# Three small VectorE operations at the end of an attention block moved to GpSimd

## The chip, the cores and the metric

The kernel runs on 1 core of one Trainium2 chip. The metric is device time of one execution in microseconds (us), the median of several executions. Less is better.

## The reference

Two layers of a diffusion backbone run over 2048 latent tokens and 256 context tokens of width 1024. In each layer one input projection is cut into three head groups; two of them are attentions:

- A, windowed attention: 6 query heads in 2 groups of 3, each group with one key and value head. A block of 128 queries sees 3 blocks of latent keys and all 256 context keys, and the softmax has one more term, a learned sink per head.
- C, neighbourhood attention: 6 heads, each query sees a window of 8 rows by 16 columns on a 32 by 64 grid, with a bias, and all context keys. There is no sink.

```python
s_sink = jnp.broadcast_to(sink.reshape(A_KV_HEADS, A_GROUP)[None, None, :, :, None, None], s_win.shape[:-1] + (1,))
p_win, p_ctx, _ = joint_softmax([s_win, s_ctx, s_sink])
o = einsum('bnkgqj,bnjkd->bnqkgd', p_win, vw) + einsum('bnkgqj,bjkd->bnqkgd', p_ctx, v_ctx)
```

Then come an output projection, a LayerNorm and an expert-choice mixture of experts, which the change does not touch.

## The kernel before, in words

Each engine executes its own instructions strictly in the order in which the program was written, and waits on semaphores where it needs another engine's result. `phase_att(l)` (L893) writes the attention of layer l. Its list of blocks is first A: 2 units (key heads) of 16 latent blocks, in the first layer also 2 context blocks each; then C: 6 units (heads) of 4 blocks, in the first layer also one context block each. A block is made of members: 3 heads in A, 4 tiles of queries in C.

The main loop takes one member per turn and writes, with a lag of up to three members between the steps: `qk` (L1040, L1041: scores, TensorE), `soft_max` (L1062: mask or bias added and the minimum taken, VectorE), `soft_exp` (L1070: exponential and its sum `ss`, ScalarE), `trans` and `trans_ctx` (L1087, L1110: transposes, TensorE), copies of the transposes into `ph` (L1199, ScalarE) and their low parts `pl` (L1190, VectorE).

Three turns after a block's last member, the generator `pv` (L1115) begins. It does one piece at each "R" of the orders ORDERA and ORDERC, two per turn: products with the values (L1145), copy to `ot` (L1151), the sink's exponential (L1153 on VectorE: sink minus minimum into `rs`; L1154 on ScalarE), transposes back (L1158), copy to `o` (L1161), the sum `ss` with the sink's term (L1163, VectorE), its reciprocal (L1165, VectorE), the two halves of the product added (L1167, VectorE, reads PSUM), the scaling of `o` (L1170, VectorE), and the store of `o` from SyncE's queue (L1172 for A, L1174 and L1178 for C).

GpSimd has two tasks in attention. For each unit of C it issues 16 small transfers that lay out a table of biases (L960 in `load_unit`), and for three of the four column groups of a unit it makes three tiles of bias from table and mask (L1002 in `bias_part`), after zeroing the two bias buffers once per layer (L990, L994). `load_unit` for the first head of C is written at the fifth block of A's second unit, that for the next head at the second block of the first one.

Of the kernel before, what the change touches and what calls it, by code (L numbers as in the profile page):

```python
# [12 lines left out]
ALU = mybir.AluOpType  # L13
# [211 lines left out]
def build(ctx, tc, t, out):  # L225
    nc = tc.nc
    V, S, P, G, SY = nc.vector, nc.scalar, nc.tensor, nc.gpsimd, nc.sync
# [665 lines left out]
    def phase_att(l):  # L893
# [6 lines left out]
        op = es.enter_context(tc.tile_pool(name="at_o", bufs=6))  # L900
# [12 lines left out]
        sink = sinks[:, l, :]  # L913
# [7 lines left out]
        for b in blist:  # L921
            nm = 3 if b[0] == "A" else (4 if b[2] < 4 else 2)
# [192 lines left out]
        def pv(b, nm):  # L1115

            kind, u, n = b
            rec = st[b]
            ph, pl = rec["ph"], rec["pl"]
            N = 128 * nm  # L1120
            v = units[kind, u]["v"]
            po = pso.tile([128, 512], F32, name="po")
            steps = []
            if kind == "A":
                steps = [(v[:, j, :], slice(9 + 3 * j, 12 + 3 * j), 0, N) for j in range(2)]
                if n >= 2:
                    a0, a1 = max(n - 1, 2), min(n + 1, NT - 1)
                    steps += [(v[:, a0 + j, :], slice(3 * j, 3 * j + 3), 0, N) for j in range(a1 - a0 + 1)]
            else:
                steps = [(v[:, j, :], slice(16 + 4 * j, 16 + 4 * j + nm), 0, N) for j in range(2)]  # L1130
                if n < 4:
                    vw = blks[b]["vw"]
                    for r in range(8):
                        a, z = ((0, 1), (0, 2), (0, 2), (1, 3), (1, 3), (2, 4), (2, 4), (3, 4))[r]
                        s0 = 2 * r + (1 if r == 7 else 0)
                        steps.append((vw[:, r, :], slice(s0, s0 + z - a), 128 * a, 128 * z))
            ns = len(steps)
            work = []
            for x, (w, s, c0, c1) in enumerate(steps):
                work.append((po[:, c0:c1], w, ph[:, s, :], x == 0, False))  # L1140
            for x, (w, s, c0, c1) in enumerate(steps):
                work.append((po[0:64, c0:c1], w[:, 0:64], pl[:, s, :], False, x == ns - 1))
            per = -(-len(work) // PVN[nm])
            for j, (o, w, r, s0, s1) in enumerate(work):
                P.matmul(o, w, r, start=s0, stop=s1, skip_group_check=True)  # L1145
                if j % per == per - 1 and j < len(work) - 1:
                    for _ in range(PVW):
                        yield
            yield
            ot = wp.tile([128, 512], F32, name="ot")  # L1150
            S.copy(ot[:, :N], po[:, :N])  # L1151
            if kind == "A":
                V.tensor_tensor(rec["rs"][:, :nm], sink[:, 3 * u:3 * u + 3], rec["mx"][:, :nm], op=ALU.subtract)  # L1153
                S.activation(rec["rs"][:, :nm], rec["rs"][:, :nm], AF.Exp, scale=-1.0)  # L1154
            yield
            px = pst.tile([128, 4, 128], F32, name="pt")
            for m in range(nm):
                P.transpose(px[:, m, :], ot[:, 128 * m:128 * m + 128], ident)  # L1158
            yield
            o = op.tile([128, 4, 64], F32, name="o")  # L1160
            S.copy(o[:, :nm, :], px[:, :nm, 64:128])  # L1161
            if kind == "A":
                V.tensor_tensor(rec["ss"][:, :nm], rec["ss"][:, :nm], rec["rs"][:, :nm], op=ALU.add)  # L1163
            yield
            V.reciprocal(rec["rs"][:, :nm], rec["ss"][:, :nm])  # L1165
            yield
            V.tensor_tensor(o[:, :nm, :], px[:, :nm, 0:64], o[:, :nm, :], op=ALU.add)  # L1167
            yield
            yield
            V.tensor_tensor(o[:, :nm, :], o[:, :nm, :], rec["rs"][:, :nm, None].to_broadcast([128, nm, 64]), op=ALU.mult)  # L1170
            if kind == "A":
                SY.dma_start(MIXA[l][128 * n:128 * n + 128, 192 * u:192 * u + 192], o[:, 0:3, :].rearrange("p m d -> p (m d)"))  # L1172
            elif n == 4:
                SY.dma_start(MIXC[l][0:256, 64 * u:64 * u + 64].rearrange("(m p) d -> p m d", p=128), o[:, 0:2, :])  # L1174
            else:
                dst = MIXC[l][256:TT, 64 * u:64 * u + 64].rearrange("(m a g b) d -> m g a b d", m=4, a=8, g=4)
                for m in range(4):
                    (G if b == blist[-1] else SY).dma_start(dst[m, n], o[:, m, :])  # L1178
            del st[b], blks[b]
# [3 lines left out]
        for i, (b, m, nm) in enumerate(mem):  # L1183
            kind, u, n = b
# [20 lines left out]
        for i in range(NM + LAG):  # L1205
            b, m, nm = mem[i - LAG]
            win, ctx_ = [], []
            for x in ORDERA if mem[min(i, NM - 1)][0][0] == "A" else ORDERC:
                if x == "R":
                    run()  # L1210
                elif x in "AaDdEe" and i >= LAG:
                    if x == "A":
                        win = trans(i - LAG)
                    elif x == "a":
                        ctx_ = trans_ctx(i - LAG)
                    elif x in "Dd":
                        copies(win if x == "D" else ctx_, b)
                    else:
                        lows(win if x == "E" else ctx_, b)
                elif x == "B" and i < NM:  # L1220
                    qk(i)
                elif x == "C" and 1 <= i <= NM:
                    soft_max(i - 1)
                elif x == "F" and 1 <= i <= NM:
                    soft_exp(i - 1)
            for x in bias_at.get(i, []):
                bias_part(*x)
            if i >= LAG and m == nm - 1:
                gens.append(pv(b, nm))
# [722 lines left out]
```

## Time and profile before

| | |
|---|---|
| runs (us) | 4326.2, 4334.8, 4321.42; median 4326.2 |
| profiled execution | 4323.15 us, span of its trace 4321.4 us |
| TensorE (matmul) busy | 3853.9 us, 89% of the span |
| VectorE busy | 2915.8 us, 67% |
| ScalarE busy | 1999.0 us, 46% |
| GpSimd busy | 783.9 us, 18%, 850 instructions |
| attention, first layer | about 630 to 1073 us from the span's start |
| attention, second layer | about 2788 to 3222 us |

Shares are means over the whole span. A kernel of many stages has a different limit in each, so what counts for a change in attention is read from the two stretches of attention alone. In the rows below PE is TensorE's matmul, PEld its weight load, DVE VectorE, ACT ScalarE, POOL GpSimd, SP SyncE; L-numbers are lines of the kernel before.

### The profile page before, as it was taken

What the parts mean: (1) busy time and instruction counts of PE and PEld (TensorE: products, weight loads), DVE (VectorE), ACT (ScalarE), POOL (GpSimd) and SP (SyncE); (2) the same over time, 40 slices, a digit from 0 to 9 for tenths busy, and PEclk for the clock granted to TensorE, in tenths of its full rate; (3) what the DMA queues carried; (4) which work ended last, traced back from release to release, by engine and by line L of the source; (5) the groups of instructions that cost most, each with busy time, mean ns of one, the idle gap of its engine ahead of it and who ended that gap; (6) DMA issues with size and microseconds to landing.
All of it is one profiled execution on the core that took longest, in us unless ns stands there. A gap on an engine that the chain in (4) does not pass through costs nothing. (4 is left out here: it accounts for less than half of the span.)

```text
span 4321.4 us, 64189 instructions
## 1 busy us (share of the span) xinstructions
PE 3853.9 (89%) x22980; PEld 3285.1 (76%) x22980; DVE 2915.8 (67%) x5836; ACT 1999.0 (46%) x3918; POOL 783.9 (18%) x850
## 2 busy tenths in 40 slices
PE   7999989999998699999978999899989918988893
PEld 5877778888885388888857888788878718888783
DVE  6555549998676366676747665499877756656576
ACT  4344338887332143343425443388763304333344
POOL 0000011052221022222210000111422201111114
PEclk9999989999998899999989999999999959999996
DMA  7666674586644878888857666645865327776796
GB/s 229 172 209 187 198 189 107 118 177 154 235 159 143 189 208 201 204 217 196 223 171 230 192 205 187 171 116 110 169 185 193 131 80 190 195 221 194 217 234 203
DMA packets 897295, 789.94 MB, mean 183 GB/s; under 512 B 125928, under 2 KB 780400, under 8 KB 893136
## 3 DMA queue, kind: packets, MB, share of 16 engines
q1 hardware_dynamic: 855744, 656.83, 56.4%
q0 software_dynamic: 41232, 129.01, 10.6%
q8 instruction: 182, 2.98, 0.3%
q14 instruction: 137, 1.12, 0.1%
HBM read 607.08 MB, written 178.48 MB: 182 GB/s over the span
## 5 line engine op out<-in xcount | busy, mean ns | idle before, releaser
L178 ACT CAST wh<-wraw 128x1024 fp32r<-128x1024 f32 x636 | 655.9, 1048 | 621.9 <-DMA wraw<-in_w_gate 278.2
L186 DVE TENSOR_TENSOR wl<-wraw,wh 128x1024 fp32r<-128x1024 f32 x636 | 754.7, 1217 | 152.2 <-ACT wh L178 152.0
L1190 DVE TENSOR_TENSOR pl<-pt,ph 128x256 fp32r<-128x256 f32 (+2 forms) x792 | 360.2, 495 | 23.0 <-ACT ph L1199 18.4
L1199 ACT CAST ph<-pt 128x256 fp32r<-128x256 f32 (+2 forms) x792 | 308.9, 445 | 99.2 <-PE pt L1087 91.3
L624 PE MATMUL gem<-hh,wh 128*128 128x512 f32 (+1 forms) x960 | 354.5, 369 | 0.0
L625 PE MATMUL gem<-hl,wh 128*128 128x512 f32 (+1 forms) x960 | 352.1, 367 | 0.0
L626 PE MATMUL gem<-hh,wl 128*128 128x512 f32 (+1 forms) x960 | 350.0, 365 | 0.0
L1070 ACT ACTIVATE p<-lg,mx 128x640 f32<-128x640 f32 (+3 forms) x408 | 331.5, 813 | 38.3 <-DVE mx L1062 36.7
L1802 PE MATMUL pa<-xh,wh 128*128 128x288 f32 (+1 forms) x1024 | 317.5, 310 | 0.0
L1804 PE MATMUL pa<-xh,wl 128*128 128x288 f32 (+1 forms) x1024 | 308.3, 301 | 0.8 <-DVE wl L186 0.8
L1803 PE MATMUL pa<-xl,wh 128*128 128x288 f32 (+1 forms) x1024 | 307.3, 300 | 0.0
L1802 PE MATMUL pu<-xh,wh 128*128 128x288 f32 (+1 forms) x1024 | 299.9, 293 | 0.0
L1804 PE MATMUL pu<-xh,wl 128*128 128x288 f32 (+1 forms) x1024 | 294.6, 288 | 0.0
L1803 PE MATMUL pu<-xl,wh 128*128 128x288 f32 (+1 forms) x1024 | 292.6, 286 | 0.0
L1666 POOL DMA_INDIRECT ACC<-y,ix x62 | 150.7, 2430 | 651.7 <-DVE y L1647 334.2
L802 PE MATMUL gem<-wh,hh 128*128 128x512 f32 x544 | 220.7, 406 | 0.6 <-ACT hh L593 0.6
L803 PE MATMUL gem<-wl,hh 128*128 128x512 f32 x544 | 217.6, 400 | 1.4 <-DVE wl L186 1.4
L804 PE MATMUL gem<-wh,hl 128*128 128x512 f32 x544 | 217.0, 399 | 0.0
L1833 PE MATMUL py<-wh,gh 128*128 128x512 f32 x512 | 205.1, 401 | 12.7 <-DVE y L1647 6.1
L1571 PE MATMUL tr<-ident,xe 128*128 128x128 f32 x512 | 89.6, 300 | 139.4 <-DVE xl L1584 91.8
L1802 PEld LDWEIGHTS pa<-xh,wh 128*128 128x128 f32 x1024 | 208.5, 204 | 3.1
L1546 POOL DMA_INDIRECT xe<-H,ix x80 | 98.2, 1228 | 619.9 <-DVE ix L1541 352.9
(352 smaller groups left out, 10103.4 us busy)
## 6 DMA issues: line engine op xcount, KB each, us to landing
wraw<-in_w_in SPq DMA_DIRECT2D x160, 512.0 KB
wraw<-in_w_gate SPq DMA_DIRECT2D x128, 512.0 KB
wraw<-in_w_up SPq DMA_DIRECT2D x128, 512.0 KB
wraw<-in_w_down SPq DMA_DIRECT2D x128, 512.0 KB
wraw<-in_w_mod SPq DMA_DIRECT2D x88, 512.0 KB
k<-KC SPq DMA_DIRECT2D x48, 576.0 KB
vw<-VS SPq DMA_DIRECT2D x192, 128.0 KB
VS<-vs SPq DMA_DIRECT2D x36, 512.0 KB
```

Source lines behind the costliest of these rows:

```text
L178: self.nc.scalar.copy(h, self.raw[i])
L186: self.nc.vector.tensor_tensor(e[1], self.raw[i], e[0].bitcast(F32), op=ALU.subtract)
L624: P.matmul(pg[:, t0:nt], wh[:, cs_], hh[:, k, t0:nt], start=(k == 0), stop=False)
L625: P.matmul(pg[:, t0:nt], wh[:, cs_], hl[:, k, t0:nt], start=False, stop=False)
L626: P.matmul(pg[:, t0:nt], wl[:, cs_], hh[:, k, t0:nt], start=False, stop=(k == KD - 1))
L802: P.matmul(pg, hh[:, k, tk], wh[:, cs_], start=(k == 0), stop=False)
L1070: S.activation(p[:, 0:768 - w0], rec["lg"][:, w0:768], AF.Exp, bias=st[b]["mx"][:, m:m + 1], scale=-1.0, accum_out=st[b]["ss"][:, m:m + 1])
L1190: V.tensor_tensor(view(st[b]["pl"]), src, view(st[b]["ph"].bitcast(F32)), op=ALU.subtract)
L1199: S.copy(view(st[b]["ph"]), src)
L1802: P.matmul(pp, wh[:, cs_], xh[:, k, :], start=(k == 0), stop=False)
L1803: P.matmul(pp, wh[:, cs_], xl[:, k, :], start=False, stop=False)
L1804: P.matmul(pp, wl[:, cs_], xh[:, k, :], start=False, stop=(k == KD - 1))
```

## The change

In `pv` three operations go from VectorE (`V`) to GpSimd (`G`). The first is also written at another place: at the start of `pv` instead of behind the products. All other work is the same.

```diff
             N = 128 * nm
+            if kind == "A":
+                G.tensor_tensor(rec["rs"][:, :nm], sink[:, 3 * u:3 * u + 3], rec["mx"][:, :nm], op=ALU.subtract)
             v = units[kind, u]["v"]
...
             if kind == "A":
-                V.tensor_tensor(rec["rs"][:, :nm], sink[:, 3 * u:3 * u + 3], rec["mx"][:, :nm], op=ALU.subtract)
                 S.activation(rec["rs"][:, :nm], rec["rs"][:, :nm], AF.Exp, scale=-1.0)
...
             if kind == "A":
-                V.tensor_tensor(rec["ss"][:, :nm], rec["ss"][:, :nm], rec["rs"][:, :nm], op=ALU.add)
+                G.tensor_tensor(rec["ss"][:, :nm], rec["ss"][:, :nm], rec["rs"][:, :nm], op=ALU.add)
             yield
             V.reciprocal(rec["rs"][:, :nm], rec["ss"][:, :nm])
...
-            V.tensor_tensor(o[:, :nm, :], o[:, :nm, :], rec["rs"][:, :nm, None].to_broadcast([128, nm, 64]), op=ALU.mult)
+            G.tensor_tensor(o[:, :nm, :], o[:, :nm, :], rec["rs"][:, :nm, None].to_broadcast([128, nm, 64]), op=ALU.mult)
```

In the changed kernel the three stand on L1122, L1164 and L1171; L1163 to L1170 of the kernel before are one line further down. The next pieces show the order in which instructions stand on GpSimd in the first layer. Before, at the start of attention (`toep` is the table of biases, `va` and `bias` the two bias buffers):

```order
L723 DMA OB0_91<-stl_5459 128x257
L960 DMA toep_7362<-in_rpb 8x16x48 x16
L990 MEMSET bias_5510 128x2048
L994 MEMSET va_8579 128x256 x3
L1002 TENSOR_TENSOR va_8579<-maskC_5509,toep_7362 128x384
L1002 TENSOR_TENSOR va_8579<-maskC_5509,toep_7362 128x512
L1002 TENSOR_TENSOR va_8579<-maskC_5509,toep_7362 128x384
L960 DMA toep_8679<-in_rpb 8x16x48 x16
```

Nothing of a block's end stands between these instructions. Now, around the first 16 transfers, in A's second unit (the numbers tell buffers apart: `rs_7059` and `rs_7135` belong to two blocks that follow each other):

```order
L1164 TENSOR_TENSOR ss_7058<-ss_7058,rs_7059 128x3
L1171 TENSOR_TENSOR o_7283<-o_7283,rs_7059 128x192
L960 DMA toep_7362<-in_rpb 8x16x48 x16
L1122 TENSOR_TENSOR rs_7220<-sinks_80,mx_7218 128x3
L1164 TENSOR_TENSOR ss_7134<-ss_7134,rs_7135 128x3
L1171 TENSOR_TENSOR o_7398<-o_7398,rs_7135 128x192
```

The same 16 transfers have moved behind the scaling of one block and ahead of the sum of the next. And now at the end of A in the first layer, where the second 16 transfers stand:

```order
L1164 TENSOR_TENSOR ss_8323<-ss_8323,rs_8324 128x3
L990 MEMSET bias_5510 128x2048
L994 MEMSET va_8580 128x256 x3
L1002 TENSOR_TENSOR va_8580<-maskC_5509,toep_7362 128x384
L1171 TENSOR_TENSOR o_8556<-o_8556,rs_8324 128x192
L1002 TENSOR_TENSOR va_8580<-maskC_5509,toep_7362 128x512
L1122 TENSOR_TENSOR rs_8498<-sinks_80,mx_8496 128x3
L1164 TENSOR_TENSOR ss_8413<-ss_8413,rs_8414 128x3
L1002 TENSOR_TENSOR va_8580<-maskC_5509,toep_7362 128x384
L960 DMA toep_8679<-in_rpb 8x16x48 x16
L1171 TENSOR_TENSOR o_8628<-o_8628,rs_8414 128x192
L1164 TENSOR_TENSOR ss_8497<-ss_8497,rs_8498 128x3
```

Before, the transfers and the bias tiles stood alone on GpSimd. Now they stand between the ends of the blocks; in both layers one group of 16 transfers has sums with the sink (L1164) of A's blocks behind it in A's second unit, and one at the passage from A to C.

## Rows read from the trace of the kernel before

**Rows 1.** Windows: stretch, PE, PEld, DVE, ACT, POOL busy (us), PEclk, DMA share, GB/s

```profile
700.00:750.00 50.00, 49.12 (x343) 43.72 (x342) 49.25 (x163) 45.56 (x142) 7.23 (x12) 1.00 0.24 68
...
3100.00:3150.00 50.00, 45.58 (x324) 41.63 (x323) 42.34 (x98) 38.65 (x96) 24.86 (x32) 0.93 0.81 163
```

**Rows 2.** Timeline of one A block: start us, us, engine, line, operation [idle before <-releaser]

```profile
716.50 0.88 DVE L1062 CUSTOM_DVE_ANT_0 lg<-lg,maskA,sinks 128x640 f32<-128x640 f32 x1
716.66 0.19 PEld L1040 LDWEIGHTS lg<-k,qa 128*128 128x128 f32 x1 [0.16 <-ACT p L1070]
...
716.85 0.23 ACT L1154 ACTIVATE rs<-rs 128x3 f32<-128x3 f32 x1
...
717.30 0.16 DVE L1163 TENSOR_TENSOR ss<-ss,rs 128x3 f32<-128x3 f32 x1
...
718.29 0.17 DVE L1165 RECIPROCAL rs<-ss 128x3 f32<-128x3 f32 x1
...
719.15 0.35 DVE L1167 TENSOR_TENSOR o<-pt,o 128x192 f32<-128x192 f32 x1
...
721.04 0.35 DVE L1170 TENSOR_TENSOR o<-o,rs 128x192 f32<-128x192 f32 x1
...
721.38 0.88 DVE L1190 TENSOR_TENSOR pl<-pt,ph 128x384 fp32r<-128x384 f32 x2
...
722.17 0.89 DVE L1062 CUSTOM_DVE_ANT_0 lg<-lg,maskA,sinks 128x640 f32<-128x640 f32 x1
```

**Rows 3.** Timeline of two C blocks of the second layer, PE and DVE

```profile
3101.83 0.55 PE L1087 MATMUL pt<-ident,p 128*128 128x128 f32 x3
...
3110.14 0.55 PE L1087 MATMUL pt<-ident,p 128*128 128x128 f32 x3
```

```profile
3104.09 1.05 DVE L1170 TENSOR_TENSOR o<-o,rs 128x256 f32<-128x256 f32 x1
...
3112.40 0.42 DVE L1170 TENSOR_TENSOR o<-o,rs 128x256 f32<-128x256 f32 x1
```

**Rows 4.** Timeline: a long L1170 in A, and PE behind it in both layers

```profile
755.30 3.23 DVE L1170 TENSOR_TENSOR o<-o,rs 128x192 f32<-128x192 f32 x1
...
759.92 0.44 PE L1110 MATMUL pt<-ident,p 128*128 128x128 f32 x2 [3.46 <-DVE pl L1190]
...
2902.10 0.44 PE L1110 MATMUL pt<-ident,p 128*128 128x128 f32 x2 [1.75 <-DVE pl L1190]
```

**Rows 5.** Timeline of POOL, first layer of attention

```profile
622.81 4.77 POOL L960 DMA_DIRECT2D toep<-in_rpb  x8
...
636.41 1.82 POOL L990 MEMSET bias<- 128x2048 f32 x1
742.77 0.81 POOL L994 MEMSET va<- 128x256 f32 x3 [104.54 <-PE po L1145]
...
746.72 9.34 POOL L960 DMA_DIRECT2D toep<-in_rpb  x16
```

**Rows 6.** Groups of POOL, by form: count | busy us, mean ns | idle before

```profile
L496 POOL TENSOR_SCALAR m<-m 128x1 f32<-128x1 f32 x68 | 64.3, 946 | 360.8 <-ACT xr L488 360.8
...
L1002 POOL TENSOR_TENSOR va<-maskC,toep 128x384 f32<-128x384 f32 x36 | 36.6, 1016 | 210.9 <-DVE mx L1062 210.9
...
L1002 POOL TENSOR_TENSOR va<-maskC,toep 128x512 f32<-128x512 f32 x18 | 23.1, 1284 | 34.9 <-DVE mx L1062 34.8
```

**Rows 7.** Timeline at the end of A, both layers: ACT and DVE

```profile
834.16 0.21 ACT L1154 ACTIVATE rs<-rs 128x3 f32<-128x3 f32 x1
...
2984.58 0.21 ACT L1154 ACTIVATE rs<-rs 128x3 f32<-128x3 f32 x1
```

```profile
841.44 0.17 DVE L1165 RECIPROCAL rs<-ss 128x3 f32<-128x3 f32 x1
...
2993.10 0.16 DVE L1165 RECIPROCAL rs<-ss 128x3 f32<-128x3 f32 x1
```

## The prediction

> **What bounds the kernel now.** I read the windows of attention first, since the change touches nothing else. In A's stretch VectorE is busy 49.25 of 50 us, TensorE 49.12 and GpSimd 7.23; in C's stretch VectorE has 42.34 and GpSimd 24.86 [rows 1]. So VectorE looks like A's limit and not like C's. A busy TensorE is no proof of a limit, because overlapping matmuls count as busy, so next I read one block in the timeline.
>
> In A, VectorE starts the same member of two blocks at 716.50 and 722.17: a block takes 5.67 us, and between these rows the timeline shows no idle time on VectorE [rows 2]. TensorE's weight loads wait once per block, 0.16 us, for an exponential whose minimum VectorE delivered late [rows 2]. So VectorE is the limit in A, but TensorE follows close behind.
>
> In C, TensorE starts the same transposes at 3101.83 and 3110.14, 8.31 us apart. In the first of these blocks L1170 on VectorE took 1.05 us, in the second 0.42 us [rows 3], and the next block of each kind keeps the same distance. VectorE may lose 0.63 us there without any change of the block's time: in C TensorE is the limit.
>
> GpSimd works ahead. The two groups of 16 transfers in the first layer ran at 622.81 and 746.72 [rows 5], the second nearly 100 us ahead of the first block that needs it. Nothing waited for them.
>
> **What leaves VectorE.** In A each of 68 blocks loses three instructions. By distances of starts, L1170 and L1153 together hold VectorE from 721.04 to 721.38, 0.34 us; L1163 takes 0.16 us by its row [rows 2]. That is 0.50 us per block. This is the upper bound of the gain: 68 x 0.50 = 34 us. The lower bound is TensorE's visible wait, 0.16 us, since without it TensorE is the limit: 60 undisturbed blocks x 0.16 = 10 us. Some short waits of matmuls hide behind weight loads that run ahead, so I take a little above the near end, 0.22 us: **60 x 0.22 = -13.2 us**.
>
> In C 54 blocks lose L1170. Rows 3 show that even its long form costs nothing, so I take **0** there. The bound is the long form's excess of 0.63 us for the 26 L1170 that the timeline shows over 0.5 us in C: -16 us, which rows 3 speak against.
>
> The long form itself is a collision. L1170 reads two tensors in SBUF, and it lasts 3.23 us at 755.30 in place of 0.35 us [rows 4, 2], while GpSimd was making bias tiles. TensorE then waited 3.46 us, and 1.75 us at the like place of the second layer [rows 4]. VectorE's other operations in attention read scores or transposes in PSUM, or one small tensor, so these two waits go: **-5.2 us**.
>
> **What GpSimd gets.** From the tiles of 384 and 512 columns, 1016 and 1284 ns, a column costs 2.1 ns and an instruction 0.21 us at the start [rows 6]. So the scaling costs about 0.61 us for 192 columns and 0.75 us for 256, and each of the two tiny ones 0.22 us; the upper bound for a tiny one is 0.95 us [rows 6]. In an undisturbed block that is 1.05 us of 5.67. Does anyone wait? ScalarE's exponential ends at 717.08, the sum can stand at 717.30, and VectorE asks for it at 718.29 [rows 2]: even at 0.95 us it would be in time. The first operation now stands at the start of `pv` and is early. The scaling can start as soon as L1167 ends, 1.54 us before L1170 started before, so the store is not late. Undisturbed blocks therefore pay **0**.
>
> **What is queued behind the 16 transfers.** This is the wait that the change adds. GpSimd no longer works ahead: each group of 16 transfers now stands behind a block's scaling, and in A the next block's sum stands behind the transfers. VectorE's reciprocal waits for that sum, and minimum and low parts of the following members are queued behind the reciprocal. A group takes 9.34 us, or 13.60 us (622.81 to 636.41) where its transfers must wait for earlier ones to land [rows 5].
>
> Second unit of A, once in each layer, told in times of the block of rows 2: L1167 ends at 719.50, the scaling takes until 720.11, the transfers until 729.45, L1122 and L1164 until 729.89. The reciprocal of the next block is due at 718.29 + 5.67 = 723.96. VectorE stands for 5.9 us, or 10.2 us with the long group. I take 6: **+12 us** for both layers. I stay near the short end though the next head's keys are loaded at the same time, because a wait of TensorE for that load's queue should vanish in the pause.
>
> End of A, first layer: the exponential of one block ends at 834.37 [rows 7]. Behind it GpSimd has L1164 0.22, zeroing 1.82 and 0.81, a tile 1.02, a scaling 0.61, a tile 1.28, L1122 0.22, L1164 0.22, a tile 1.02 (this comes to 841.59), the transfers 9.34, a scaling 0.61 and the L1164 in question 0.22: 851.76. Its reciprocal is due at 841.44 [rows 7]: **+10.3 us**, with the long group 14.6.
>
> End of A, second layer: the exponential ends at 2984.79; L1164 0.22, transfers 9.34, scaling 0.61 and L1164 0.22 make 2995.18, due at 2993.10 [rows 7]: **+2.1 us**, with the long group 6.3.
>
> In C no reciprocal waits for GpSimd, since C has no sink, and the tiles are needed some five members (10 us) after they are written. I take 0, with the last block's scaling of 0.75 in place of 0.36 us in each layer: **+0.8 us**.
>
> **Sum.** -13.2 - 5.2 + 12 + 10.3 + 2.1 + 0.8 = +6.8 us on the profiled execution's 4323.15 us, 4330 us. The median of the runs stands 3.05 us above that execution, so the predicted median is **4333 us**, 0.16% above 4326.2. A measurement of this kernel can tell about 0.3% (13 us) from no change, so the forecast is no measurable change.
>
> A rule of the Trainium skill speaks against the whole idea: GPSIMD Engine Reference, section 4.1 Engine selection, sends elementwise work on tiles to VectorE because GpSimd is about twice as slow with two inputs. Here the 384-column row gives no direct pair, but 1.05 us of GpSimd for 0.50 us of VectorE agrees in size. By that rule alone the change would lose where GpSimd's time is on the path, which is the third rival.
>
> **The rivals.**
> - *VectorE's full share comes out of A* (0.14). If TensorE's waits are all due to VectorE, A's 68 blocks give 34 us in place of 13.2: 4312 us, faster. For it: no idle time of VectorE. Against it: TensorE's 49.12 of 50 us [rows 1].
> - *The transfers take long* (0.22). They are now issued beside the loads of the next head's keys. With 13.6 us each, the four places lose 4.3 us more: +17, 4350 us, slower. It decides from some 11 us per group. For it: the group at 622.81, beside such loads. Against: the one at 746.72.
> - *GpSimd's own slowness is on every block's path* (0.06). If a tiny operation with its two hand-overs takes more than 1.05 us (718.29 less 0.16 less 717.08), VectorE waits in each block; at 1.3 us that is 68 x 0.25 = 17 us: 4350 us, slower.
> - *The change gives A nothing* (0.10), because TensorE is the limit there as in C. Without the 13.2 us it ends at 4346 us, slower.
>
> **How the numbers follow.** The forecast has 0.48; its own spread is 4322 to 4344. The range 4313 to 4351 takes in the full gain of A below and the long transfers above. Faster by over 0.3% (under 4313): 0.14. Slower by over 0.3% (over 4339): the three slower rivals, less what they share with gains elsewhere, 0.34. Within: 0.52.
>
> **What the profile after would show.** In A a block of some 5.45 us; VectorE idle before the minimum or the low parts, TensorE without the 0.16 us wait. No L1170-like operation over 0.5 us on VectorE, no waits of 3.46 and 1.75 us behind it. Four pauses in which VectorE's reciprocal waits for GpSimd's sum, about 6, 10, 6 and 2 us, each behind L960 on GpSimd. C at 8.31 us per block as before. The prediction is wrong if these four pauses are missing, if A's block falls to 5.2 us, or if VectorE waits for GpSimd in every block.

## The result, and the profile after the change

Six runs of the changed kernel gave a median of 4352.8 us (4349.7 to 4355.23), six of the kernel before 4329.82 us: a ratio of 1.0055, interval 1.0041 to 1.0069. The change costs 23 us. The forecast was 4333 us with a range up to 4351. The profiled execution took 4354.22 us, 31.07 us more than the profiled one of before; 8 of these lie in how the two executions stand to their medians. Lines from L1120 on have moved by one or two: L1122 is the subtraction, L1164 the sum, L1166 the reciprocal, L1168 the sum of halves, L1171 the scaling.

First the windows that answer to [rows 1] (stretch, PE, PEld, DVE, ACT, POOL busy, PEclk, DMA share, GB/s):

```profile
700.00:750.00 50.00, 49.37 (x346) 44.25 (x345) 46.73 (x133) 46.09 (x144) 8.12 (x29) 1.00 0.20 60
3100.00:3150.00 50.00, 45.11 (x321) 41.00 (x320) 39.73 (x93) 37.95 (x93) 26.35 (x35) 0.93 0.78 162
```

VectorE is relieved as planned, 46.73 in place of 49.25 us of 50. The timeline of VectorE and of the weight loads shows what an undisturbed block of A makes of it:

```profile
788.68 0.88 DVE L1062 CUSTOM_DVE_ANT_0 lg<-lg,maskA,sinks 128x640 f32<-128x640 f32 x1
...
794.36 0.88 DVE L1062 CUSTOM_DVE_ANT_0 lg<-lg,maskA,sinks 128x640 f32<-128x640 f32 x1
```

```profile
794.63 0.19 PEld L1040 LDWEIGHTS lg<-k,qa 128*128 128x128 f32 x1 [0.17 <-ACT p L1070]
```

The same member comes 5.68 us later, where it was 5.67 us before, and the weight load still waits 0.17 us for an exponential [rows 2]. The freed half microsecond bought nothing. In C the same transposes on TensorE start 8.31 and 8.33 us apart, against 8.31 before [rows 3]:

```profile
3129.28 0.55 PE L1087 MATMUL pt<-ident,p 128*128 128x128 f32 x3
...
3137.59 0.55 PE L1087 MATMUL pt<-ident,p 128*128 128x128 f32 x3
...
3145.92 0.55 PE L1087 MATMUL pt<-ident,p 128*128 128x128 f32 x3
```

The loss is in the reciprocal. The view of line L1166 gives its waits in all, and the timeline of VectorE each of them:

```profile
L1166 DVE RECIPROCAL rs<-ss x122: 155/167/176, 648.7 to 3242.9; 128x3 f32<-128x3 f32 x68, 128x4 f32<-128x4 f32 x48, 128x2 f32<-128x2 f32 x6
its engine sat idle before it (us, times) until:
  POOL ss L1164: 41.8, 5
```

```profile
766.92 0.18 DVE L1166 RECIPROCAL rs<-ss 128x3 f32<-128x3 f32 x1 [12.68 <-POOL ss L1164]
844.74 0.18 DVE L1166 RECIPROCAL rs<-ss 128x3 f32<-128x3 f32 x1 [1.39 <-POOL ss L1164]
859.51 0.18 DVE L1166 RECIPROCAL rs<-ss 128x3 f32<-128x3 f32 x1 [12.56 <-POOL ss L1164]
2933.87 0.17 DVE L1166 RECIPROCAL rs<-ss 128x3 f32<-128x3 f32 x1 [12.23 <-POOL ss L1164]
3017.45 0.18 DVE L1166 RECIPROCAL rs<-ss 128x3 f32<-128x3 f32 x1 [2.98 <-POOL ss L1164]
```

The four places that the prediction named are there, with 41.8 us in place of 24.4. What GpSimd and SyncE did before the first of them:

```profile
749.77 0.51 POOL L1171 TENSOR_TENSOR o<-o,rs 128x192 f32<-128x192 f32 x1 [2.23 <-DVE o L1168]
750.22 6.60 POOL L960 DMA_DIRECT2D toep<-in_rpb  x11
757.12 0.60 POOL L960 DMA_DIRECT2D toep<-in_rpb  x1 [0.30 <-DMA toep<-in_rpb]
...
762.71 0.59 POOL L960 DMA_DIRECT2D toep<-in_rpb  x1 [2.46 <-DMA toep<-in_rpb]
...
765.93 0.59 POOL L960 DMA_DIRECT2D toep<-in_rpb  x1 [1.25 <-DMA toep<-in_rpb]
766.53 0.21 POOL L1122 TENSOR_TENSOR rs<-sinks,mx 128x3 f32<-128x3 f32 x1
766.70 0.19 POOL L1164 TENSOR_TENSOR ss<-ss,rs 128x3 f32<-128x3 f32 x1
```

```profile
752.17 2.63 SPq L946 DMA_DIRECT2D k<-KC  x4
```

The group begins right behind the scaling, and 1.95 us later SyncE issues the next head's keys. Eleven transfers are issued without a pause; from then on each waits until an earlier one has landed. The group takes 16.3 us (750.22 to 766.52). Before, this same group took 13.60 us at the start of attention, and the group that ran at this time, at 746.72, was the next head's and took 9.34 us [rows 5].

**Where the time is.** The table takes one member's minimum (L1062, counted from the start of attention) in both profiled executions, with start times from VectorE's timeline.

| member | before, us | after, us | difference | what lies between |
|---|---|---|---|---|
| 1 | 630.70 | 630.77 | +0.07 | |
| 10 | 652.98 | 648.74 | -4.24 | first keys of attention |
| 61 | 747.09 | 743.28 | -3.81 | undisturbed A |
| 81 | 789.90 | 794.36 | +4.46 | pause of 12.68 |
| 141 | 903.84 | 922.36 | +18.52 | pauses of 1.39 and 12.56 |
| 216 | 1063.39 | 1077.27 | +13.88 | C |
| 217 | 2788.34 | 2805.02 | +16.68 | end of C, the rest of the layer |
| 241 | 2841.12 | 2855.05 | +13.93 | first keys |
| 301 | 2958.64 | 2980.55 | +21.91 | pause of 12.23 |
| 335 | 3032.42 | 3058.61 | +26.19 | pause of 2.98, first head of C |
| 408 | 3209.60 | 3237.73 | +28.13 | C |

Something is gained at both starts. Before, TensorE waited 4.06 us there for keys. GpSimd had issued its first group from 622.81 us on [rows 5], and by the trace the last of these transfers landed at 645.48 us; the wait ended at 645.13. After, the group is not there and the wait is 0.83 us. Of the kernel before:

```profile
645.13 0.66 PE L1040 MATMUL lg<-k,qa 128*128 128x384 f32 x1 [4.06 <-DMA k<-KA]
```

and of the changed kernel:

```profile
642.27 0.41 PE L1040 MATMUL lg<-k,qa 128*128 128x384 f32 x1 [0.83 <-DMA k<-KA]
```

### The profile page after: what moved, and what is told of

It reads as the page before. It is cut to its first block, busy times and chain, and to the rows that moved or that the text cites. A ratio compares the mean times of both kernels' runs of the same rounds, so it can differ in the third digit from the quotient of the medians.

```text
span 4352.4 us, 64435 instructions
## 1 busy us (share of the span) xinstructions
PE 3851.2 (88%) x22980; PEld 3284.1 (75%) x22980; DVE 2864.6 (66%) x5578; ACT 1997.8 (46%) x3918; POOL 874.6 (20%) x1108
## 3 DMA queue, kind: packets, MB, share of 16 engines
q8 instruction: 182, 2.98, 0.3%
## 5 line engine op out<-in xcount | busy, mean ns | idle before, releaser
L1087 PE MATMUL pt<-ident,p 128*128 128x128 f32 x1224 | 205.7, 281 | 25.8 <-DVE o L1168 24.8
```

## The experiments

Theory 1: the loss is the sum that stands behind a group of transfers, and an undisturbed block of A gains nothing. Theory 2: GpSimd's slower work and its hand-overs lie on every block's path. The kernel before had a median of 4322 to 4323 us in the runs of this section, and ratios are to it. The expectations of the scaling alone, the two small operations alone, the spread transfers and the three operations on no engine still count from the 4330 us of the result; they are read here as differences.

**Scaling alone on GpSimd**

```diff
 # in the kernel before
-            V.tensor_tensor(o[:, :nm, :], o[:, :nm, :], rec["rs"]..., op=ALU.mult)
+            G.tensor_tensor(o[:, :nm, :], o[:, :nm, :], rec["rs"]..., op=ALU.mult)
```

> Only the scaling of the output goes to GpSimd; the subtraction and the sum with the sink's exponential stay on VectorE. Theory 1 (the loss is five pauses, 41.8 us together, in which VectorE's reciprocal waits for a sum that GpSimd issues behind a group of 16 transfers, and A's block gains nothing): no reciprocal waits for GpSimd any more, the pauses are gone, while what the change gained stays (3.5 us at the start of each attention, and about 5 us of waits behind long L1170). With some 2.8 us more at the end of each layer that makes 4330 - 7 - 5 + 5 = about 4323 us, A's block 5.67 us. Theory 2 (GpSimd's slower work and its hand-overs lie on every block's path): the scaling is 0.51 of the 0.90 us of GpSimd's work per block, so more than half of the loss of 23 us stays, about 4343 us.

Measured: 4308.38 us, ratio 0.9968 (0.9958 to 0.9978), faster than before by twice what theory 1 said. No reciprocal waits for GpSimd. So the larger part of the work that moved, 0.51 of 0.90 us per block, costs nothing on GpSimd; theory 2 falls. One wait behind a group is left, at the end of A in the first layer, where VectorE needs a tile of bias that GpSimd makes behind the group:

```profile
843.75 0.83 DVE L1062 CUSTOM_DVE_ANT_0 lg<-lg,bias 128x640 f32<-128x640 f32 x1 [4.98 <-POOL bias L1002]
```

**The two small operations alone on GpSimd**

```diff
 # in the changed kernel
-            G.tensor_tensor(o[:, :nm, :], o[:, :nm, :], rec["rs"]..., op=ALU.mult)
+            V.tensor_tensor(o[:, :nm, :], o[:, :nm, :], rec["rs"]..., op=ALU.mult)
```

> Only the subtraction and the sum go to GpSimd; the scaling stays on VectorE. Theory 1: the sum still stands behind the transfers wherever GpSimd cannot run ahead, so the pauses stay, some 42 us, and the long L1170 come back with up to 5 us: 4350 to 4358 us. But nothing of a block's end now holds GpSimd back before the transfers except the two small operations, so a group may start a few us earlier. Theory 2: 0.39 of 0.90 us of GpSimd's work, 10 of the 23 us: about 4340 us.

Measured: 4334.14 us, ratio 1.0026 (1.0016 to 1.0035). The loss of 12 us is nearer to theory 2's 10 us than to theory 1's 20 to 28 us, but the cause is theory 1's: the five pauses are there, so the sum alone makes them. They come to 23.6 us and not 42. The reason is in the first of them:

```profile
746.68 0.20 POOL L1164 TENSOR_TENSOR ss<-ss,rs 128x3 f32<-128x3 f32 x1 [4.99 <-ACT rs L1155]
747.30 9.49 POOL L960 DMA_DIRECT2D toep<-in_rpb  x16 [0.42 <-issue]
756.75 0.26 POOL L1122 TENSOR_TENSOR rs<-sinks,mx 128x3 f32<-128x3 f32 x1
756.91 0.25 POOL L1164 TENSOR_TENSOR ss<-ss,rs 128x3 f32<-128x3 f32 x1
```

```profile
757.20 0.18 DVE L1166 RECIPROCAL rs<-ss 128x3 f32<-128x3 f32 x1 [3.62 <-POOL ss L1164]
```

Without the scaling ahead of it the group starts 2.92 us earlier (747.30, not 750.22). When SyncE issues the keys, at 751.78 us, GpSimd is 4.5 us into the group and not 1.95 us, and the group takes 9.49 us; the pause is 3.62 us. The scaling alone is free, and yet with the sums it adds 9 us to this pause, because it holds the group back until shortly before the keys. Where the keys are issued early in the group all the same, at the end of A in the first layer (group from 835.57, keys from 838.55 us), the pause is still 13.93 us.

**The group one block earlier, all of the change kept**

```diff
 # load_toep(u): the 16 transfers, taken out of load_unit (not shown)
+                if at == ustart["A", 1] + 3:
+                    load_toep(0)          # the 16 transfers of C's first table
                 if at == ustart[kind, u] + (4 if kind == "A" else 1) and x < len(ulist):
                     load_unit(*ulist[x])  # keys and values as before
```

> All of the change is kept; only the group of 16 transfers for C's first table, in the middle of A, is issued one block of A earlier, while the keys that are loaded beside it stay where they are. If the group is long because its transfers share the time with these keys (16.3 us against 9.5 us in the run with the sums alone, where it began 2.9 us earlier): the group takes 9.4 to 10 us and the pause in the middle of A falls from 12.7 and 12.2 us to about 6 in each layer, 13 us less than the change as made: 1.002 to before. Rival (the group is long for another reason, its place behind the scaling or the wait of GpSimd itself): pauses of 12 us stay and the ratio is 1.005.

Measured: 4332.56 us, ratio 1.0020 (1.0007 to 1.0032), as expected if the keys make the group long. The group is over before the keys are issued and takes 9.5 us in both layers (740.82 to 750.35 in the first). The pauses in the middle of A are 4.47 and 6.01 us:

```profile
750.75 0.18 DVE L1174 RECIPROCAL rs<-ss 128x3 f32<-128x3 f32 x1 [4.47 <-POOL ss L1172]
```

```profile
2907.89 0.18 DVE L1174 RECIPROCAL rs<-ss 128x3 f32<-128x3 f32 x1 [6.01 <-POOL ss L1172]
```

So the company of the keys is what makes the group and the pause long, and 6 us, the prediction's value, is the pause without them.

**The transfers spread over the members, all of the change kept**

```diff
-                    G.dma_start(tv[:, b], bass.AP(...))
+                    pend.append((tv[:, b], bass.AP(...)))
...
+            for _ in range(1 if mem[min(i, NM - 1)][0][0] == "A" else 3):
+                if pend:
+                    G.dma_start(*pend.pop(0))
             for x in bias_at.get(i, []):
```

> All of the change is kept, but the 16 transfers of a toep table are not issued in one group: one after each member of A (1.9 us), three after each member of C. Theory 1: GpSimd is held for 0.6 us at a time in A, the sum is in time, the pauses are gone and the gains stay: about 4323 us, as with the scaling alone on GpSimd. Theory 2: nothing of GpSimd's work on the path changes, so the time stays at about 4353 us.

Measured: 4308.46 us, ratio 0.9967 (0.9954 to 0.9980). Two pauses of together 5.3 us are left of 41.8. The same instructions run on the same engines; only the place of the transfers in GpSimd's order differs, and a loss of 0.55% becomes a gain of 0.33%.

**A's three operations on no engine**

```diff
 # in the kernel before, for A
-                V.tensor_tensor(rec["rs"]..., sink..., rec["mx"]..., op=ALU.subtract)
-                S.activation(rec["rs"][:, :nm], rec["rs"][:, :nm], AF.Exp, scale=-1.0)
+                S.activation(rec["rs"][:, :nm], rec["mx"][:, :nm], AF.Exp, scale=-1.0)
...
-                V.tensor_tensor(rec["ss"]..., rec["ss"]..., rec["rs"]..., op=ALU.add)
...
+            if kind != "A":
                 V.tensor_tensor(o[:, :nm, :], o[:, :nm, :], rec["rs"]..., op=ALU.mult)
```

> The kernel before with A's three operations left out and put on no engine: the exponential of the sink reads the minimum, the sum is not made and A's output is not scaled, so A's output is another. GpSimd's order is that of before. It shows what A can gain at most when VectorE is relieved of 0.50 us per block. If TensorE limits A's block (theory 1): the block stays at 5.67 us and only the waits behind long L1170 in A go, about 4325 us. If VectorE limits it, as my prediction had it: 5.45 us or less per block, 13 us for 60 blocks and 5 us of waits, 4312 us, down to 4296 us if all 0.50 us come out.

Measured: 4315.5 us, ratio 0.9989 (0.9979 to 0.9999). The block stays:

```profile
784.60 0.88 DVE L1062 CUSTOM_DVE_ANT_0 lg<-lg,maskA,sinks 128x640 f32<-128x640 f32 x1
...
790.27 0.88 DVE L1062 CUSTOM_DVE_ANT_0 lg<-lg,maskA,sinks 128x640 f32<-128x640 f32 x1
```

5.67 us with nothing moved to GpSimd and 0.50 us taken from VectorE: in an undisturbed block the three operations are worth nothing, wherever they run. The 6.5 us that the kernel gains lie mostly where L1170 collided with GpSimd (below). Here GpSimd works ahead again, and the first group is back at 623.8 us; the starts gain nothing.

**Less for TensorE, in the changed kernel with spread transfers and in the kernel before**

```diff
             for x, (w, s, c0, c1) in enumerate(steps):
+                if kind == "A" and n >= 2 and x < 2:
+                    continue
                 work.append((po[0:64, c0:c1], w[:, 0:64], pl[:, s, :], False, x == ns - 1))
```

> The kernel with the whole change and the transfers spread over the members, and with two of TensorE's ten value products in each block of A left out (the low parts against the context's two groups of values, 0.18 us each by the trace, 0.35 us per block); A's output loses that small part. If TensorE limits A once VectorE is relieved (theory 1): the block falls from 5.67 to some 5.35 to 5.45 us, where VectorE's own work (0.947 of the time between 740 and 752 us, 5.37 us per block) becomes the limit; 64 blocks by 0.25 are 16 us, about 4292 us where before is 4322. Rival (neither engine but a chain of waits between them sets the block): 5.67 us and about 4308 us.

Measured: 4296.74 us, ratio 0.9941 (0.9925 to 0.9957), 11.7 us less than with the products.

> The kernel before with the same two products of each block of A left out, VectorE as before. If VectorE stands at the same limit as TensorE in the kernel before (theory 1: both at 5.67 us, so that relief of either alone is worth nothing): the block stays at 5.6 to 5.67 us and the time within 4 us of before. Rival (TensorE alone limits A, VectorE had room all along): 5.32 to 5.4 us, 64 by 0.3 = 19 us, about 4303 us.

Measured: 4318.1 us, ratio 0.9987 (0.9977 to 0.9998). The block falls in both, and by the same: to 5.53 us with the change and 5.54 us without. With the change:

```profile
784.25 0.89 DVE L1063 CUSTOM_DVE_ANT_0 lg<-lg,maskA,sinks 128x640 f32<-128x640 f32 x1
...
789.78 0.89 DVE L1063 CUSTOM_DVE_ANT_0 lg<-lg,maskA,sinks 128x640 f32<-128x640 f32 x1
```

Without it, and the busy times of this kernel between 783 and 817 us:

```profile
783.67 0.87 DVE L1062 CUSTOM_DVE_ANT_0 lg<-lg,maskA,sinks 128x640 f32<-128x640 f32 x1
...
789.21 0.87 DVE L1062 CUSTOM_DVE_ANT_0 lg<-lg,maskA,sinks 128x640 f32<-128x640 f32 x1
```

```profile
783.00:817.00 34.00, 33.21 (x235) 30.17 (x233) 34.00 (x105) 32.65 (x93) 0.00 (x0) 1.00 0.19 54
```

Neither expectation holds in full. TensorE limits the block at 5.67 us, since less work for it shortens the block and less for VectorE doesn't. But 0.35 us less gave only 0.14: something else holds at 5.53. In the kernel before, VectorE did all its work in 5.54 us, so its full row in [rows 1] still held 0.13 us of slack that no idle time showed. With the change VectorE has room. The waits between 783 and 817 us (waiter, releaser, us in total, times, longest) tell who came late, here without the change and with it:

```profile
PEld pt L1110 <- DVE pl L1192: 2.4, 7, 0.4
```

```profile
PEld lg L1041 <- ACT p L1071: 2.1, 6, 0.3
DVE pl L1194 <- ACT ph L1203: 1.5, 6, 0.3
```

Without the change TensorE's weight loads now wait for VectorE. With it they and VectorE wait for ScalarE, which itself waits for nothing in this stretch. So ScalarE looks like the limit at 5.53 us, but no run took work from it, so this is read and not shown.

**The transfers on SyncE, with the change and in the kernel before**

```diff
-                    G.dma_start(tv[:, b], bass.AP(...))
+                    SY.dma_start(tv[:, b], bass.AP(...))
```

> All of the change is kept, but the toep transfers are issued on SyncE's queue behind the keys of the same unit, so that nothing of attention on GpSimd stands behind them. Theory 1 (the loss is the sum behind the transfers): no pauses, ratio to before 0.997 as in the run with spread transfers, about 4308 us where before is 4322. In C the next block's loads stand behind the 16 issues on SyncE, some 10 us, which may cost 1 to 2 us per unit if they are then late. Theory 2 (GpSimd's slower work on each block's path): no better than the change itself, 1.005.

Measured: 4417.65 us, ratio 1.0219 (1.0206 to 1.0233). The pauses are gone but for one of 1.4 us, as theory 1 said, and yet the kernel is slower by 95 us.

> The kernel before, with nothing moved off VectorE: only the toep transfers are issued on SyncE's queue behind the keys of the same unit, so they no longer run beside the first keys of attention. Theory 1 (the start of attention gains 3.5 us in each layer because the transfers no longer compete with the first keys): first members 3.5 us earlier in each layer, A's block 5.67 us, the long L1170 as before: 4322 - 7 = about 4315 us, ratio 0.9985. Rival (the start gains because VectorE or GpSimd has less to do there): ratio 1.000.

Measured: 4421.29 us, ratio 1.0224 (1.0210 to 1.0238). Both expectations were far off. The starts do gain (member 10 comes 4.0 us earlier than before in the second of these), but in C the queue itself is the trouble, here in the kernel before:

```profile
845.58 3.43 SPq L946 DMA_DIRECT2D k<-KC  x4
849.05 0.59 SPq L954 DMA_DIRECT2D vx<-VS  x1
849.85 17.89 SPq L960 DMA_DIRECT2D toep<-in_rpb  x16
...
868.81 0.40 SPq L979 DMA_DIRECT2D qc<-QC  x1
```

```profile
872.43 0.66 PE L1040 MATMUL lg<-k,qc 128*128 128x384 f32 x1 [5.86 <-DMA qc<-QC]
```

The 16 issues hold SyncE for 17.9 us, and the queries behind them come late. By the members' times it costs some 10 us for most of the groups. The cure moved the same fault to another queue.

**GpSimd paced, VectorE as before**

```diff
 # in the kernel before, at the start of pv; gp is read by nobody
+            if kind == "A":
+                G.tensor_tensor(rec["gp"][:, :nm], sink[:, 3 * u:3 * u + 3], rec["mx"][:, :nm], op=ALU.subtract)
```

> The kernel before, with VectorE's work untouched, and one additional GpSimd operation per block of A: sink minus minimum into a tile that nobody reads, at the place where the change has its first one. Nobody waits for GpSimd, but GpSimd cannot run ahead of A any more, so the first group of transfers leaves the start of attention. If the gain of the runs without pauses (13.6 us) is due to where GpSimd's transfers and tiles fall in time and not to VectorE's relief: the starts gain 3.5 us each, and the long L1170 in the middle of A goes where its companion on GpSimd has moved (3.5 us): 0.9975 to 0.9985, 4311 to 4316 us where before is 4322. Rival (relieving VectorE, and with it the collision of L1170 with GpSimd, is what gains): 0.9995 to 1.000.

Measured: 4314.14 us, ratio 0.9977 (0.9967 to 0.9988). One more operation that does nothing makes the kernel 9 us faster: it only keeps GpSimd from running ahead (the first group is issued at 742.47 us in place of 622.81). So, by the medians, most of the 13.6 us that the good variants gain comes from where GpSimd's transfers and tiles fall, not from VectorE's relief. Against the kernel with spread transfers, 3.5 us of the rest lie at the end of A in the first layer (members 112 to 122), where the scaling on VectorE meets GpSimd's tiles:

```profile
839.41 6.28 DVE L1172 TENSOR_TENSOR o<-o,rs 128x192 f32<-128x192 f32 x1
```

```profile
839.01 1.02 POOL L1002 TENSOR_TENSOR bias<-maskC,toep 128x384 f32<-128x384 f32 x1
839.97 0.20 POOL L1122 TENSOR_TENSOR gp<-sinks,mx 128x3 f32<-128x3 f32 x1
840.13 2.22 POOL L1002 TENSOR_TENSOR bias<-maskC,toep 128x512 f32<-128x512 f32 x2
842.32 3.15 POOL L1002 TENSOR_TENSOR va<-maskC,toep 128x384 f32<-128x384 f32 x3
```

**Scaling alone on GpSimd, and the transfers spread:** the first edit and the fourth together, on the kernel before.

> Scaling alone on GpSimd and the transfers spread over the members, as a candidate for the best of them. Theory 1 says that after the pauses are gone nothing is left for the spreading to win in A: about 0.997, as with either edit alone. Where the group at the end of A in the first layer still meets other loads (the scaling-only run loses 6.7 us between its members 112 and 122, the spread one 4.7 us), spreading may give back 2 us: 0.9965.

Measured: 4307.9 us, ratio 0.9963 (0.9950 to 0.9975). This is the lowest of the kernels with all the work in them, but its interval overlaps those of the two edits alone. Either edit makes a version faster than both kernels of this case; together they give nothing more that can be told apart.

## Why the prediction was wrong, step by step

- **What bounds A, and the gain of 13.2 us.** This step failed. The prediction said "VectorE is the limit in A" because no idle time stood between its rows. TensorE was the limit: the block is 5.67 us with VectorE's work of before, with the change, and with the three operations on no engine; it is shorter only with less for TensorE. The lower bound failed too: TensorE's visible wait of 0.16 us [rows 2] was put down to a late minimum of VectorE, and with VectorE relieved it is still 0.17 us. The term is 0, not -13.2. The rival "The change gives A nothing" had this right, with its reason. It and the rival "The transfers take long" came true together, each with only part of the loss.
- **The pauses, 24.4 us.** Right in mechanism and in all four places (the end of the first layer's A has two in a row), mis-sized: 41.8 us. This is the larger miss, 17.4 us. In the middle of A the prediction took 6 us each and had 10.2 us with a long group; it was 12.68 and 12.23. It saw that the next head's keys are loaded at the same time and stayed at the short end all the same. The group's 13.60 us beside keys in [rows 5] was the nearer row, since in the changed kernel the group and the keys follow the same block (750.22 and 752.17 us). At the end of A, 13.95 and 2.98 us stand against 10.3 and 2.1.
- **The start of attention, not priced.** The prediction moved the group away from 622.81 and asked who waits for it there ("Nothing waited for them"), but not who had waited beside it: TensorE, 4.06 us. The differences of the table are -4.2 us in the first layer and -2.7 in the second; the paced kernel, and the one before with the transfers on SyncE, show that the place of the group does it.
- **Contended L1170, -5.2 us.** Right in kind, too small. With the three operations on no engine, the difference to before falls by 5.3 us at the place in the first layer (members 61 to 76, +0.14 to -5.19) and by 2.1 us at that in the second (members 268 to 274). The changed kernel, by the table, gains 4.4 and 4.3 us beside the pauses there; what makes the other 2.2 us in the second layer is open. The paced kernel loses the wait in the middle of A too, with the scaling still on VectorE, because GpSimd's tiles stand elsewhere.
- **GpSimd's durations.** 0.19 us for a small operation, 0.51 and 0.61 us for a scaling, against 0.22, 0.61 and 0.75 in the prediction. Undisturbed blocks wait for none of them, as forecast. The Trainium skill (GPSIMD Engine Reference, section 4.1 Engine selection) puts GpSimd at about twice VectorE's time for operations with two inputs; here 0.51 stands against 0.35 us [rows 2], 1.5 times, and it decided nothing: the scaling alone on GpSimd is a gain.
- **C, 0.** Right for its blocks, 8.31 to 8.33 us, but one place was missed. [Rows 3] show that a scaling of 1.05 us costs nothing, and the prediction took that for all long ones (26 by its count, 25 by the timeline). In the first layer of the kernel before one lasted 3.25 us:

```profile
954.39 3.25 DVE L1170 TENSOR_TENSOR o<-o,rs 128x256 f32<-128x256 f32 x1
```

  The changed kernel gains 3.05 us there (members 161 to 169), and the kernels with the scaling alone, with the transfers spread and with both gain 3.0. Where the scaling stays on VectorE and lasts 2.5 to 4.0 us (two small operations alone, paced, A's three on no engine), the difference to before is -1.5 to +1.1 us. Between heads of the second layer some 4 us are lost between members 301 and 335 and 2 more after them; part of it is the last pause.

By the differences, 6.8 us of the sum become 6.8 + 13.2 (A) + 17.4 (pauses) - 6.9 (starts) - 3.5 (beside the pauses in A) - 3.0 (C, first layer) = 24.0 us, against 31.07 between the two profiled executions. The rest of some 7 us stays open. By the table it lies outside A: 2.8 us between the layers (member 216 to 217), 2.9 us behind member 408, and in C of the second layer. Other kernels of this study lie between -4.8 and +4.7 us at the first of these places and between -3.9 and +4.8 us at the second, so two single executions can't settle it.

## What to carry to other kernels

Before work goes to a quiet engine, list everything in that engine's order that may block it, and ask whether a result with a due time would stand behind it; here a sum of 0.19 us cost up to 12.7 us behind 16 transfers, and either leaving the sum where it was or spreading the transfers turned the loss into a gain. An engine that runs ahead also decides what its transfers collide with, so any new dependence moves them: price the place they leave and the place they come to. Full busy time without idle rows is no proof of a limit; take a little work from each engine and see whether the period moves.

## What was not expected of the hardware

- A scaling on VectorE that reads two tensors in SBUF lasted 6.28 us in place of 0.35, until GpSimd had ended seven instructions in a row (839.01 to 845.47 us in the paced kernel's rows). The Trainium skill (SBUF — State Buffer, section SBUF: two separate sides) says that of two such operations the one that starts first has the shared port for the whole instruction; the trace agrees on who waits, since GpSimd's first tile began 0.40 us earlier, but here VectorE was not let in between GpSimd's instructions either. It is not always so, and who starts first does not always decide: the 3.23 us of [rows 4] began at 755.30, 0.78 us before GpSimd's first tile (756.08), while the last transfers were still being issued, and ended at 758.53, before the third tile did (759.37).
- After the pause of 12.68 us the granted clock was 0.51 between 768 and 772 us, the level of 1.2 GHz, after TensorE had stood for 11.95 us. Three transposes then took 0.90 us in place of 0.49. The first line is the window, with the clock third from its end:

```profile
768.00:772.00 4.00, 3.80 (x17) 3.61 (x17) 3.50 (x9) 3.20 (x9) 0.73 (x3) 0.51 0.35 66
```

```profile
754.26 0.49 PE L1087 MATMUL pt<-ident,p 128*128 128x128 f32 x3
768.20 0.90 PE L1087 MATMUL pt<-ident,p 128*128 128x128 f32 x3 [11.95 <-DVE o L1168]
771.03 0.84 PE L1087 MATMUL pt<-ident,p 128*128 128x128 f32 x3
773.64 0.49 PE L1087 MATMUL pt<-ident,p 128*128 128x128 f32 x3
```

- A group of 16 transfers holds the engine that issues it for 9.3 to 16.3 us on GpSimd, by what else is loaded meanwhile (before, after and with the group earlier), and for 17.0 to 18.8 us on SyncE (both kernels).
